# An account that orders VectorE's work charges other durations, follows a forced finish, and the conditioning loads of layer 0's pair passes are spread 6,6,6,6,1

## The chip, the cores and the metric

The kernel runs on one core of a Trainium2 chip. The metric is the device time of one launch in microseconds (us). A kernel is timed in several runs, and their median is used; beside them stands one profiled execution, whose trace gives all the durations below.

TensorE (PE) multiplies matrices, VectorE (DVE) and ScalarE (ACT) do elementwise work, GpSimd (POOL) does next to nothing here, and SyncE's queue (SP) issues almost all transfers. Each engine works through its own queue in order and waits where an instruction needs something that is not there yet.

## The reference

Two layers over 1024 prompt rows and 32 rows of a running stream, with `D_MODEL` = 1024 and `D_FF` = 4096, all in float32:

```python
for i in range(DEPTH):                                   # DEPTH = 2
    mod = jax.nn.silu(c) @ w_ada[i] + b_ada[i]           # conditioning
    sh1, sc1, gt1, sh2, sc2, gt2 = jnp.split(mod[:, None, :], N_MOD, axis=-1)
    h = rmsnorm(x, g_norm[i, 0]) * (1 + sc1) + sh1
    if i % N_MIXERS == 0:                                # layer 0
        mix, v = sgu_mixer(h, ...)
    else:                                                # layer 1
        mix = pool_mixer(h_ext, L, pool_w_grp[j], pool_scale[j])
    x = x + gt1 * rmsnorm(mix, g_norm[i, 1])
    h = rmsnorm(x, g_norm[i, 2]) * (1 + sc2) + sh2
    f = jnp.square(jax.nn.relu(h @ ffn_w_up[i])) @ ffn_w_down[i]
    x = x + gt2 * rmsnorm(f, g_norm[i, 3])
```

The pooling mixer of layer 1 takes trailing means over 2, 4, 8 and 16 rows, subtracts the row itself and multiplies by a 256x256 matrix for each of four groups.

## The kernel before

**Tiles.** The rows are cut into three tiles (`TILES`): tile 0 and tile 1 of 384 rows, tile 2 of 256 prompt rows and the 32 stream rows (288 columns). Activations are held transposed, features on the partitions. Every float32 product is made of three matmuls: each operand is split into a high part (`wh`, `hh`, `fh`; a copy by ScalarE) and a low part (`wl`, `hl`, `fl`; a subtraction by VectorE), and `products` (L1042 ff.) issues high*high, high*low and low*high. So each 128x1024 piece of weights costs one transfer of 512 KB into one of three `raw` buffers, one ScalarE copy and one VectorE subtraction before TensorE may use it.

**Passes.** The channel MLP runs in passes (`passes`): a layer, a first chunk `c` of 512 hidden features, the tiles, and the number of chunks taken together. In layer 0: two passes of tile 0, three of tile 1, five passes c = 3 to 7 of tiles 0 and 1 together (the pair passes, `pair_item`; their up-projection has seven block products in place of eight, with operands that `combos` prepares), and four passes of tile 2 with two chunks each. Layer 1 is alike: a pass of tile 0, two of tile 1, six pair passes c = 2 to 7, four passes of tile 2. Up-projections write the tiles `pf` (`pfa`, `pfb`, `pfc` in pair passes), down-projections write `pg`, which VectorE adds to `acc`.

**The conditioning.** `w_ada` comes in pieces of 512 KB too, through the same `raw` buffers and in the same stream of loads as the weights. `do_ada` multiplies and adds a piece on VectorE (instructions `aa<-raw,csil,aa`); every four pieces of a column block end in two transposes and two sums (`part`), and a small matmul (`ada`, L649) folds the sums. The list `rest` holds the pieces that are still to come; `some_ada(n)` puts the next n of them into the stream. After the weights of each pair pass of layer 0 five pieces are put in, after those of layer 1 two (L422).

**Fillers.** The work between the matmuls of one stage and the next is written as generators in the list `fillers`: the residual and its norm (`residual`, `Stat`), the pooling (`to_pool`), the modulation (`modulate`, `apply`), `combos`. `pull` runs the next step of the first or second filler. For layer 1, `ffn1_0` and `ffn1_1` take tile 0 and tile 1 from the end of the last pair pass of layer 0 to the operands `hh` and `hl` of layer 1's first passes: residual of layer 0 (statistics `pn_r2_0_0x` and `pn_r2_0_1x` on TensorE), windows on VectorE (`win`), matmuls `pp` (L1940), their norm (`pn_rp`), a second residual (`pn_r1_1_0x`, `pn_r1_1_1x`), and the modulation. In the trace the statistics of the second residual are `pn_r_0x` and `pn_r_1x`. While these run, TensorE has the four passes of tile 2 of layer 0.

**The account.** The program is written out in one order for each engine when it is built, and that order is decided by two running sums in `time`. `tick` adds the matmuls' time to `time["pe"]`; every VectorE operation issued through `tt`, `stt`, `ts` or `turn32` adds a fixed time and its elements divided by a rate to `time["dve"]` (L71 to L87). `weave`, called after each group of matmuls, takes a step of the weight stream unless `stream_waits` holds it back (for weights not needed soon, where fillers are there and `dve` is over 1.0 ahead of `pe`; for conditioning, 0.5 ahead), and then pulls fillers while `dve` is behind `pe`. A filler that waits for something gives a number, and `pull` opens it again only once `pe` has come to the larger of the two sums plus that number. Folds of the conditioning are put off in the same way (`defer`).

**Forced finishes.** Where a stage needs a filler's result, `finish(tag)` (L816) pulls until that filler is done, whatever the account says; so do `run_ffn` before the first pass of each tile and `pair_item` (for `combos`, and for tile 2 ahead of the down-projection of the last pair pass).

Of the kernel before, what the change touches and what calls it, by code (L numbers as in the profile page):

```python
# [35 lines left out]
def tile_stream_encoder_step(  # L36
# [25 lines left out]
    nc = tc.nc  # L62
# [5 lines left out]
    time = {"pe": 0.0, "dve": 0.0}  # L68
# [5 lines left out]
    def on_dve(op, fixed, rate):  # L74
        def run(out, *args, **kw):
            n = 1
            for k in out.shape[1:]:
                n *= k
            time["dve"] += fixed + n / rate
            return op(out, *args, **kw)  # L80

        return run

    tt = on_dve(nc.vector.tensor_tensor, 0.16, 930.0)
    stt = on_dve(nc.vector.scalar_tensor_tensor, 0.16, 840.0)
    ts = on_dve(nc.vector.tensor_scalar, 0.1, 930.0)
    turn32 = on_dve(nc.vector.transpose, 0.1, 930.0)  # L87

    def pool(name, **kw):
        return ctx.enter_context(tc.tile_pool(name=name, bufs=1, reuse_waits="tile", **kw))  # L90
# [52 lines left out]
    def ps_ms(name):  # L143
        return psum.tile([P, 512], F32, tag="pm", bufs=3, name=name)
# [207 lines left out]
    def w_chunk(n):  # L352
        l, c, tiles, m = passes[n]
        for j in range(4 * m):
            f = 4 * c + j
            add_w(
                ("up", n, j),
                ffn_w_up[l][:, f * P : (f + 1) * P].rearrange("(k p) f -> p k f", p=P),
                (8, P),
                ("one", "two")[j % 2] if tiles == PAIR else "w",  # L360
            )
        w = 256 // m
        for q in range(4 * m):
            add_w(
                ("dn", n, q),
                ffn_w_down[l][c * 512 : (c + m) * 512, q * w : (q + 1) * w].rearrange(
                    "(j p) d -> p j d", p=P
                ),
                (4 * m, w),
            )  # L370
# [15 lines left out]
    def some_ada(n):  # L386
        for _ in range(min(n, len(rest))):
            add, l, j = rest.pop(0)
            add(l, j)
# [29 lines left out]
    for n, (l, c, tiles, m) in enumerate(passes):  # L419
        w_chunk(n)  # L420
        if tiles == PAIR:
            some_ada((5, 2)[l])  # L422
        elif l == 0 and tiles != [NT - 1] and c > 0:
            some_ada(c + 1 if tiles == [1] else 2)
    some_ada(99)
# [120 lines left out]
    def ada_finish(l, sl, view):  # L546

        nk = 2 * view.shape[1]
        m = mod[:, l, 2 * sl : 2 * sl + nk, :].rearrange("p (s h) v -> p s h v", h=2)
        b = bT[:, l * 48 + 2 * sl : l * 48 + 2 * sl + nk].rearrange("p (s h) -> p s h", h=2)  # L550
        tt(out=m, in0=view, in1=b.unsqueeze(3).broadcast_to([P, nk // 2, 2, NV]), op=ALU.add)
        which, k0 = sl // 4, 2 * (sl % 4)
        slot = {1: (0, 0), 2: (1, 1), 4: (2, 2), 5: (3, 3)}.get(which)
        if slot is not None:
            cf, gi = slot
            for v in range(NV):
                stt(
                    out=coef[:, l, cf, v, k0 : k0 + nk],
                    in0=mod[:, l, 2 * sl : 2 * sl + nk, v],
                    scalar=1.0 if cf in (0, 2) else 0.0,  # L560
                    in1=g_of(l, gi)[:, k0 : k0 + nk],
                    op0=ALU.add,
                    op1=ALU.mult,
                )
# [40 lines left out]
    def do_ada(l, sl, q, r, w):  # L605
        nq = w // 128
        if q == 0:
            aas = [
                work.tile([P, 512], F32, tag="aa", bufs=2, name=f"aa{l}_{sl}_{w}_{i}")
                for i in range(nq // 2)  # L610
            ]
            ada_acc[0] = [aas[v * nq // 4][:, v * w % 512 :][:, :w] for v in range(NV)]
        aa = ada_acc[0]
        for c in range(8 // nq):
            for v in range(NV):
                x = r[:, c * w : (c + 1) * w]
                k = csil[:, 8 // nq * q + c, v : v + 1]
                if q == 0 and c == 0:
                    with tc.issue_after(last_lo[("v", 1, 3)].ins):
                        ts(aa[v], x, k, None, op0=ALU.mult)  # L620
                else:
                    stt(out=aa[v], in0=x, scalar=k, in1=aa[v], op0=ALU.mult, op1=ALU.add)
        if q < nq - 1:
            return


        ns = nq // 2
        i = sl * ns % 4
        if i == 0 and state["folds"]:
            run_deferred(True)  # L630
        for v in range(NV):
            turned = r[:, v * w : (v + 1) * w]
            turn32(turned, aa[v])
            time["dve"] += 0.16 + w / 840.0
            nc.vector.tensor_reduce(
                out=part[:, i : i + ns, v],
                in_=turned.rearrange("p (s b m) -> p s b m", s=ns, m=32),
                op=ALU.add,
                axis=AX.X,
            )  # L640
        if i + ns < 4:
            return
        state["folds"] = 1

        def fold():
            state["folds"] = 0
            pa = ps_ms(f"ada{l}_{sl}")
            for c in range(4):
                mm(  # L649
                    pa[32 * c : 32 * c + 32, :16],  # L650
                    quad,
                    part.rearrange("p s v (h c) -> p c (s v h)", c=4)[:, c],
                    start=True,
                    stop=True,
                    tile_position=(0, 32 * c),
                    skip_group_check=True,
                )
            y = pa[:, :16].rearrange("p (s v h) -> p s h v", s=4, v=NV)
            ada_finish(l, (sl + 1) * ns - 4, y)

        defer(fold, fold_lag[0])
# [3 lines left out]
    def defer(step, us=None):  # L665

        at = 0.0 if us is None else max(time["pe"], time["dve"]) + us
        deferred.append((at, step))

    def run_deferred(force=False):  # L670
        n = len(deferred)
        while n > 0 and (force or deferred[0][0] <= time["pe"]):
            deferred.pop(0)[1]()
            n -= 1
# [39 lines left out]
    def stream_step():  # L714
# [17 lines left out]
        if kind == "w":  # L732
            do_w(key, r)
        elif kind == "wide":
            do_ada(*key, r, 512)
        elif kind == "ada":
            if k < first_ada:
                do_ada_pe(*key, r)
            else:
                do_ada(*key, r, 256)  # L740
        else:
            do_x(key, r)
# [35 lines left out]
    def pull(force=False):  # L778

        def open_(f):
            return force or gates.get(f[0], 0.0) <= time["pe"]

        if sticky:
            f = sticky[-1]
            if not open_(f):
                return False
            sticky.pop()
        else:  # L790
            f = next((f for f in list(fillers)[:2] if open_(f)), None)
            if f is None:
                return False
        try:
            step = next(f[1])
        except StopIteration:
            fillers.remove(f)
            return True
        if step is True:
            sticky.append(f)  # L800
        elif step is not False:
            gates[f[0]] = max(time["pe"], time["dve"]) + step
        return True
# [12 lines left out]
    def finish(tag):  # L816
        while any(f[0] == tag for f in fillers):
            pull(True)


    def spread(t, ss, tag, out, dg):
# [729 lines left out]
    def pair_item(p, after, ends):  # L1551
# [48 lines left out]
        def up(jp):  # L1600
# [10 lines left out]
            if jp == 0:  # L1611
                flush()
                finish("combos")
# [56 lines left out]
        if passes[p + 1][2] != PAIR:  # L1670
            finish(f"ffn{l}_{NT - 1}")
            fillers.append(late_norm.pop())
# [277 lines left out]
    def run_ffn(l, after):  # L1950
        for p, (pl, c, tiles, m) in enumerate(passes):
            if pl != l:
                continue
            ends = [t for t in tiles if not any(q[0] == l and t in q[2] for q in passes[p + 1 :])]
            if tiles == PAIR:
                pair_item(p, after, ends)
                continue
            for t in tiles:
                if c == 0:
                    if any(f[0] == f"ffn{l}_{t}" for f in fillers):  # L1960
                        flush()
                    finish(f"ffn{l}_{t}")
                ffn_item(p, t, after if t in ends else None)
# [158 lines left out]
```

## Time and profile before

| what | value |
|---|---|
| median of 3 runs | 2157.3 us (2157.04 to 2158.1) |
| the profiled execution, its time | 2154.9 us |
| the profiled execution, its span | 2153.1 us |
| instructions in the span | 32925 |
| DVE busy | 1560.3 us, 72% of the span |
| ACT busy | 1041.6 us, 48% of the span |
| DMA read and written | 274.76 MB and 30.66 MB |

The span runs from the first to the last instruction of the trace; the execution's own time is 1.8 us longer. Times in the views are counted from the start of the span. In the view of waits each row names who waited, for whom, the sum in us, how often, and the longest. In the view of windows each row has the stretch, its length and then for each engine the busy time with the number of instructions, the clock granted to TensorE as a share of full speed, and the DMA engines' share and rate. In the timeline each row has start, duration, engine, line, operation, tiles and shapes. VectorE's and TensorE's instructions overlap a little: the distance from one start to the next is shorter than the duration of one.

### The profile page before, as it was taken

The numbers are of one execution on the slowest core, as the hardware profiler recorded it, in microseconds if no ns is written. First come the engines' busy times: TensorE is split into PE (matmuls) and PEld (weight loads), VectorE is DVE, ScalarE is ACT, GpSimd is POOL, SyncE is SP. The second block draws the span as 40 slices with busy tenths as digits, with TensorE's granted clock in tenths as the row PEclk, the third lists the DMA queues.
The fourth block names the chain that finished last, engine by engine and source line by source line (L and its number), as shares of the span: only waits on it lengthen the run. The fifth ranks groups of instructions, "written<-read, shape, count | busy, mean of one in ns | idle before, by whom it ended". The sixth has DMA issues, their size and how long they took to land.

```text
span 2153.1 us, 32925 instructions
## 1 busy us (share of the span) xinstructions
PE 2102.8 (98%) x12858; PEld 2032.5 (94%) x12858; DVE 1560.3 (72%) x2756; ACT 1041.6 (48%) x1833; POOL 22.4 (1%) x44
## 2 busy tenths in 40 slices
PE   8999999999999999999998999896999999999998
PEld 6878999999999999999998999896999999999998
DVE  6778837567778857878777887849677768579554
ACT  5634431233456545334455756555445454365555
POOL 0000000000000000000000000000000000001100
PEclk9999999999999999999999999998999999999999
DMA  8576524353445443334335775643342323238873
GB/s 290 169 256 210 179 81 136 97 163 109 122 129 167 138 147 121 105 98 128 108 122 146 214 221 145 191 131 104 89 142 90 91 86 101 69 113 224 203 188 92
DMA packets 424050, 307.59 MB, mean 143 GB/s; under 512 B 47023, under 2 KB 387287, under 8 KB 423893
## 3 DMA queue, kind: packets, MB, share of 16 engines
q1 hardware_dynamic: 422964, 304.19, 47.2%
q8 instruction: 101, 1.65, 0.3%
q0 software_dynamic: 896, 1.28, 0.2%
q14 instruction: 57, 0.46, 0.1%
q10 hardware_dynamic: 32, 0.01, 0.0%
HBM read 274.76 MB, written 30.66 MB: 142 GB/s over the span
## 4 chain that ended last, share of the span: by engine, by line
PE 90%; DVE 5%; DMA 2%; ACT 2%; issue 1%; DVEq 0%; ACTq 0%
PE pg L1048 10%; PE pg L1047 10%; PE pg L1049 10%; PE pf L1047 5%; PE pf L1048 5%; PE pf L1049 5%; PE pu L1047 3%; PE pu L1049 3%; PE pu L1048 3%; PE po L1047 3%; PE po L1049 3%; PE po L1048 3%; PE pfa L1586 3%; PE pfa L1588 3%; PE pfa L1587 3%; PE pv L1073 2%
## 5 line engine op out<-in xcount | busy, mean ns | idle before, releaser
L1047 PE MATMUL pg<-fh,wh_dn 128*128 128x384 f32 (+1 forms) x968 | 314.7, 326 | 0.9 <-DVE acc L80 0.9
L1048 PE MATMUL pg<-fl,wh_dn 128*128 128x384 f32 (+1 forms) x968 | 312.9, 323 | 0.0
L1049 PE MATMUL pg<-fh,wl_dn 128*128 128x384 f32 (+1 forms) x968 | 311.9, 323 | 0.0
L80 DVE TENSOR_TENSOR wl_dn<-raw,wh_dn 128x1024 fp32r<-128x1024 f32 x148 | 181.1, 1224 | 140.3 <-ACT wh_dn L533 92.9
L1047 PE MATMUL pf<-hh,wh_up 128*128 128x288 f32 (+1 forms) x832 | 262.4, 316 | 10.0 <-ACT hh L1007 8.4
L1048 PE MATMUL pf<-hl,wh_up 128*128 128x288 f32 (+1 forms) x832 | 260.8, 314 | 0.0
L1049 PE MATMUL pf<-hh,wl_up 128*128 128x288 f32 (+1 forms) x832 | 260.1, 313 | 0.0
L533 ACT ACTIVATE wh_dn<-raw 128x1024 fp32r<-128x1024 f32 x148 | 156.7, 1059 | 152.2 <-PE pf L1048 65.1
L80 DVE SCALAR_TENSOR_TENSOR aa<-raw,csil,aa 128x512 f32<-128x512 f32 (+1 forms) x364 | 206.2, 620 | 4.5 <-DMA raw<-in_w_ada_dram 4.4
L80 DVE TENSOR_TENSOR acc<-acc,pg 128x384 f32<-128x384 f32 (+1 forms) x256 | 134.7, 531 | 85.7 <-PE pg L1049 84.4
L1047 PEld LDWEIGHTS pg<-fh,wh_dn 128*128 128x128 f32 x968 | 181.5, 188 | 2.6 <-DVE acc L80 1.3
L1048 PEld LDWEIGHTS pg<-fl,wh_dn 128*128 128x128 f32 x968 | 181.7, 188 | 1.0 <-DVE fl L80 0.2
L1049 PEld LDWEIGHTS pg<-fh,wl_dn 128*128 128x128 f32 x968 | 181.6, 188 | 0.0
L533 ACT ACTIVATE wh_up<-raw 128x1024 fp32r<-128x1024 f32 x104 | 110.2, 1059 | 127.1 <-PE pg L1048 76.2
L80 DVE TENSOR_TENSOR wl_up<-raw,wh_up 128x1024 fp32r<-128x1024 f32 x104 | 126.8, 1220 | 61.1 <-ACT wh_up L533 60.6
L1047 PEld LDWEIGHTS pf<-hh,wh_up 128*128 128x128 f32 x832 | 158.5, 191 | 12.6 <-ACT hh L1007 9.2
L1048 PEld LDWEIGHTS pf<-hl,wh_up 128*128 128x128 f32 x832 | 158.4, 190 | 1.1 <-DVE hl L80 0.9
L1049 PEld LDWEIGHTS pf<-hh,wl_up 128*128 128x128 f32 x832 | 158.8, 191 | 0.1
L1047 PE MATMUL pg<-fx,wh_dn 128*128 128x288 f32 (+1 forms) x392 | 121.8, 311 | 0.0
L1048 PE MATMUL pg<-fx,wh_dn 128*128 128x288 f32 (+1 forms) x392 | 121.7, 311 | 0.0
L1049 PE MATMUL pg<-fx,wl_dn 128*128 128x288 f32 (+1 forms) x392 | 121.4, 310 | 0.0
L1047 PE MATMUL po<-ush,wh_o 128*128 128x384 f32 (+1 forms) x288 | 92.6, 322 | 0.0
(408 smaller groups left out, 5112.3 us busy)
## 6 DMA issues: line engine op xcount, KB each, us to landing
raw<-in_ffn_w_up_dram SPq DMA_DIRECT2D x148, 512.0 KB, 4.0
raw<-in_ffn_w_down_dram SPq DMA_DIRECT2D x148, 512.0 KB, 4.1
raw<-in_w_ada_dram SPq DMA_DIRECT2D x90, 512.0 KB, 4.2
raw<-in_sgu_w_in_dram SPq DMA_DIRECT2D x40, 512.0 KB, 4.0
xd<-acc SPq DMA_DIRECT2D x8, 1536.0 KB, 7.4
raw<-in_sgu_w_out_dram SPq DMA_DIRECT2D x24, 512.0 KB, 3.6
xo_r<-xd SPq DMA_DIRECT2D x32, 384.0 KB, 4.1
vd<-vt SPq DMA_DIRECT2D x32, 256.0 KB, 4.4
```

Of the source, the lines that this page charges most:

```text
L80: return op(out, *args, **kw)
L533: act(out=wh, in_=r, func=AF.Copy)
L1047: mm(ps[:, :n], wh, rh, start=i == 0, stop=False)
L1048: mm(ps[:, :n], wh, rl, start=False, stop=False)
L1049: mm(ps[:, :n], wl, rh, start=False, stop=i == last)
L1073: mm(ps[:m, :], a_h, wh[:, o : o + 512], start=k == 0, stop=False)
L1586: mm(ps[:, :n], wh[:, o], rh, start=first and k == 0, stop=False, skip_group_check=True)
L1587: mm(ps[:, :n], wh[:, o], rl, start=False, stop=False, skip_group_check=True)
L1588: mm(ps[:, :n], wl[:, o], rh, start=False, stop=k == HK - 1, skip_group_check=True)
```

## The change

The account's charges become 0.07 + n/950 for `tensor_tensor` (n elements per partition), 0.13 + n/950 for `scalar_tensor_tensor`, 0.13 + n/1900 for `tensor_scalar` and 0.06 + n/880 for the transpose; the `part` sums are charged 0.06 + n/950. For 1024 columns the subtraction's charge goes from 1.261 to 1.148 us, for 512 columns the multiply-add's from 0.770 to 0.669 us. After a forced finish `pe` is set to at least `dve` less 3.0. And the pair passes c = 3, 4, 5 and 6 of layer 0 put in six pieces of conditioning each and the pass c = 7 one, 25 in all as before; layer 1 keeps two. No operation or transfer of the kernel is added or removed; what changes is the order in which the instructions of each engine are written out, and with it ScalarE's function table is loaded 18 times where it was 16.

```diff
-    tt = on_dve(nc.vector.tensor_tensor, 0.16, 930.0)
-    stt = on_dve(nc.vector.scalar_tensor_tensor, 0.16, 840.0)
-    ts = on_dve(nc.vector.tensor_scalar, 0.1, 930.0)
-    turn32 = on_dve(nc.vector.transpose, 0.1, 930.0)
+    tt = on_dve(nc.vector.tensor_tensor, 0.07, 950.0)
+    stt = on_dve(nc.vector.scalar_tensor_tensor, 0.13, 950.0)
+    ts = on_dve(nc.vector.tensor_scalar, 0.13, 1900.0)
+    turn32 = on_dve(nc.vector.transpose, 0.06, 880.0)
...
         if tiles == PAIR:
-            some_ada((5, 2)[l])
+            some_ada(2 if l else 6 if c < 7 else 1)
...
             turn32(turned, aa[v])
-            time["dve"] += 0.16 + w / 840.0
+            time["dve"] += 0.06 + w / 950.0
...
     def finish(tag):
         while any(f[0] == tag for f in fillers):
             pull(True)
+        time["pe"] = max(time["pe"], time["dve"] - 3.0)
```

## The prediction

> **What bounds the kernel now.** The page first: TensorE is busy almost all the time, so only what makes it wait, or slows it, can be won.
>
> ```profile
> span 2153.1 us, 32925 instructions
> PE 2102.8 (98%) x12858; PEld 2032.5 (94%) x12858; DVE 1560.3 (72%) x2756; ACT 1041.6 (48%) x1833; POOL 22.4 (1%) x44
> ```
>
> Some 50 us of the span are idle. The view of waits, for TensorE alone, names what ended them.
>
> ```profile
> PE pn_r_1x L920 <- ACT sc_r_1x L873: 12.5, 1, 12.5
> PE pf L1047 <- ACT hh L1007: 8.4, 2, 4.3
> PE ada L649 <- DVE part L635: 5.8, 2, 5.5
> ...
> PE pn_r_0x L920 <- ACT sc_r_0x L873: 3.1, 1, 3.1
> ...
> PE pf L1047 <- ACT wh_up L533: 1.4, 2, 0.7
> PE pfa L1586 <- ACT wh_up_A L491: 1.3, 1, 1.3
> ```
>
> `pn_r_0x` and one `hh` wait are the entry of tile 0 into layer 1, `pn_r_1x` and the other that of tile 1: 3.1 + 12.5 + 8.4 = 24.0 us in which TensorE has nothing left to do and the filler has not come through. The 5.5 us are a fold of conditioning that stands on TensorE's queue ahead of sums VectorE has not made. The timelines of both engines show it:
>
> ```profile
> 1145.89 0.29 PE L1048 MATMUL pf<-hl,wh_up 128*128 128x288 f32 x1
> 1151.69 0.31 PE L649 MATMUL ada<-part,quad 128*32 128x16 f32 x8 [5.50 <-DVE part L635]
> ```
>
> ```profile
> 1146.94 0.55 DVE L80 TENSOR_TENSOR acc<-acc,pg 128x384 f32<-128x384 f32 x1
> 1147.41 0.74 DVE L80 SCALAR_TENSOR_TENSOR aa<-raw,csil,aa 128x512 f32<-128x512 f32 x1
> 1148.08 0.56 DVE L80 TENSOR_TENSOR sq_rf<-sq_rf 128x384 f32<-128x384 f32 x1
> 1148.56 1.30 DVE L80 STREAM_TRANSPOSE raw<-aa 128x512 f32<-128x512 f32 x2
> ...
> 1150.27 1.27 DVE L635 TENSOR_REDUCE part<-raw 128x16 f32<-128x512 f32 x2
> ```
>
> Each of the three stops also costs time afterwards. The view by windows, behind each:
>
> ```profile
> 1152.00:1157.00 5.00, 5.00 (x20) 5.00 (x21) 2.45 (x6) 1.55 (x2) 0.00 (x0) 0.51 0.80 224
> 1157.00:1162.00 5.00, 5.00 (x40) 5.00 (x39) 3.36 (x4) 3.94 (x7) 0.00 (x0) 1.00 0.76 215
> 1380.00:1386.00 6.00, 6.00 (x19) 5.56 (x20) 5.99 (x12) 3.00 (x6) 0.00 (x0) 0.54 0.12 35
> 1386.00:1391.00 5.00, 5.00 (x30) 5.00 (x30) 2.26 (x3) 2.78 (x6) 0.00 (x0) 1.00 0.00 0
> 1479.00:1485.00 6.00, 6.00 (x21) 5.64 (x20) 6.00 (x12) 3.00 (x6) 0.00 (x0) 0.54 0.00 0
> ```
>
> The granted clock is 0.51 to 0.54 after each. In 5 us TensorE does 20 matmuls where it then does 40: 2.5 us lost. In 6 us it does 19 and 21 where 30 in 5 us would give 36: 2.8 and 2.5 us. Together 7.8 us.
>
> Whether VectorE has room to do the fillers earlier, and the matmuls' pace, is in four longer windows:
>
> ```profile
> 950.00:1000.00 50.00, 50.00 (x290) 50.00 (x290) 35.45 (x55) 23.20 (x43) 0.00 (x0) 1.00 0.34 106
> 1150.00:1300.00 150.00, 148.07 (x1099) 147.49 (x1100) 118.59 (x163) 93.62 (x153) 0.00 (x0) 0.98 0.72 210
> 1313.00:1373.00 60.00, 58.19 (x412) 55.38 (x410) 59.25 (x89) 41.51 (x71) 0.00 (x0) 1.00 0.65 193
> 2000.00:2050.00 50.00, 50.00 (x379) 49.90 (x378) 26.37 (x32) 25.51 (x39) 5.84 (x10) 1.00 0.79 198
> ```
>
> While TensorE works on tile 2 from 1150 to 1300, VectorE is busy 118.59 of 150 us, 79%; from 1313 to 1373 it is full, 59.25 of 60, and TensorE still loses under 2 us. The work is there to be moved from the full stretch into the slack one. A matmul of 384 columns takes 50/290 = 0.172 us, one of 288 columns 50/379 = 0.132 us.
>
> **The change part by part.** The two built programs have the same matmuls, VectorE operations and transfers; what stands where differs, and I read it from the changed program's order. VectorE's work I add up by start-to-start distances, from its full stretch:
>
> ```profile
> 1341.71 0.46 DVE L80 TENSOR_TENSOR fx<-r,fx 128x288 fp32r<-128x288 f32 x1
> 1342.08 0.97 DVE L80 TENSOR_TENSOR win1p<-win1p 128x786 f32<-128x786 f32 x1
> 1342.97 0.55 DVE L80 SCALAR_TENSOR_TENSOR r_rp<-q_rp,r_rp 128x384 f32<-128x384 f32 x1
> ...
> 1345.82 0.95 DVE L80 SCALAR_TENSOR_TENSOR acc<-win1p,acc 128x768 f32<-128x768 f32 x1
> 1346.69 0.61 DVE L80 SCALAR_TENSOR_TENSOR acc<-acc,coef,r_rp 128x384 f32<-128x384 f32 x1
> 1347.22 1.22 DVE L80 TENSOR_TENSOR wl_dn<-raw,wh_dn 128x1024 fp32r<-128x1024 f32 x1
> 1348.35 0.45 DVE L80 TENSOR_TENSOR fl<-r,fh 128x288 fp32r<-128x288 f32 x1
> ```
>
> That is 0.37 us for 288 columns, 0.89 for a window, 0.87 for 768 columns, 0.53 for a multiply-add of 384 and 1.13 for a weight's low part; the fences above give 0.47 for an addition of 384 and 0.67 for a multiply-add of 512. The new charges are these distances (1.148 for the weight, where the old account had 1.261), so the account finds VectorE behind TensorE more often and draws fillers earlier.
>
> *Entry into layer 1.* `pn_r1_1_0x` now stands 408 matmuls of 288 columns and 22 of 384 ahead of the first `pf1_0_0` (408 x 0.132 + 22 x 0.172 = 57.6 us), `pn_r1_1_1x` 386 of 384 columns ahead of the first `pf1_0_1` (66 us); before, only the statistics' own few matmuls lay between. Behind such a statistic VectorE owes 2 + 16 multiply-adds, 18 x 0.53 = 9.5 us, ScalarE eight copies beside them: covered several times over. Removed: 24.0 us.
>
> *The last fold of conditioning.* With one piece left for c = 7, the sums of `ada1_9` now precede that pass's first addition of `pg`, and its fold stands 156 matmuls of 384 columns earlier. Removed: 5.5 us. In its place one matmul of `pf0_0_2_0` stands there ahead of it and waits for a weight copy; 0 to 1.3 us, part of the pass-start term below.
>
> *The clock.* Without the three stops the 7.8 us of half clock go as well. Removed in all: 24.0 + 5.5 + 7.8 = 37.3 us.
>
> *New waits.* I laid VectorE's instructions end to end from the last place where its queue runs empty, against TensorE's matmuls from the same place. On the order of before such a sum gives 10.9 us for the recorded 12.5 and 4.8 for the 5.5.
>
> (a) Tile 2 of layer 0. From the read of `pg0_2_2_4` to `fl0_4_2_7`: 12 weights (13.6), 17 multiply-adds of 384 (9.0), 12 of 288 columns (4.4), 10 windows (8.9), 7 of 768 columns (6.1), 4 additions of 384 (1.9), a copy: 44.0 us. TensorE needs it after 294 matmuls of 288 columns (38.8), 8 of the pooling, and 2 more (0.3): the row
>
> ```profile
> 1302.45 2.58 PE pp L1940 x8
> ```
>
> adds 2.6, 41.7 in all. VectorE is 2.3 us late, and everything of layer 0's `acc` and `fl` queues behind it. Bounds 0 (ScalarE and TensorE interleave) and 4.4, if the 2.1 us by which `sm_rp_0` is late come on top; I take 2.3, since the full stretch above let TensorE lose 1.8 us in 60.
>
> (b) The first matmuls of `pfb1_3_0` are written into the down-projection of pass c = 2 of layer 1, 38 matmuls of 384 columns (6.5 us) behind `pg1_2_0_1`. Their weight `S31` comes behind five additions of 384 (2.4), four multiply-adds of 512 (2.7), three halves of a weight at some 0.6 (1.8), one weight (1.1) and nine short pieces at 0 to 0.37: 8.0 to 11.3, late by 1.5 to 4.8; I take 3.3, the middle. What is late next are the matmuls `pp2` behind it. After it the clock may fall: 0 or 2.6 us (the mean above), and as the waits of 0.7 and 1.3 us left it at 1.00 while 3.1 + 4.1 lowered it, I take 2.6.
>
> (c) The gating stage. Ahead of `usl1_0_1` 22.5 us stand on VectorE's queue against 20.7 on TensorE's, ahead of `usl5_2_1` 13.6 against 12.3: 1.8 + 1.3 = 3.1. ScalarE switches its table twice more, by this row at 1.28 us each:
>
> ```profile
> L1389 ACT ACT_TABLE_LOAD x3 | 3.8, 1283 | 0.1
> ```
>
> Bounds 0 and 3.1 + 2.6 = 5.7; I take 3.1, as ScalarE has half its time free.
>
> (d) Starts of the pair passes. A sixth piece is four multiply-adds and a quarter of two transposes and two sums, 2.7 + 0.6 = 3.3 us of VectorE ahead of the next pass's weights. Beside TensorE's 1.3 us above, ScalarE waits there for a transfer:
>
> ```profile
> ACT wh_up_A L491 <- DMA raw<-in_ffn_w_up_dram: 66.1, 9, 15.5
> ```
>
> Four starts: at worst 13.2, at best the present 1.3 + 1.4 go (-2.7); I take 1.5, near the wait that is recorded.
>
> Sum: -37.3 + 2.3 + 3.3 + 2.6 + 3.1 + 1.5 = -24.5 us. The profiled execution took 2154.9 us (span 2153.1 and 1.8 around it), which gives 2130.4; it lies 2.4 below the median of the runs shown, 2157.3, and on that scale I forecast 2133 us. With every added term at its bound: 37.3 + 2.7 gained is 2117; 4.4 + 4.8 + 2.6 + 5.7 + 13.2 = 30.7 added is 2151.
>
> The row says that a stop of 5.5 us or more costs about 2.6 us afterwards. The Trainium skill, "TensorE: Matmul & The Clock Gate", Part 1, has the clock fall to half after an idle window of about 3.4 us that runs free of the kernel, and rise after one busy window. An estimate from its figure would put 1.7 us on each stop, 5.1 for the three, and the forecast at about 2135; against the change it says that (b), at 3.3 us, may or may not lower the clock. Here the trace shows 2.5 to 2.8, and the trace decides.
>
> **The rivals.** *No new wait counts* (0.15): small waits are taken up by what lies around them, as the order of before had some of 2 to 3 us in tile 2's passes that no row shows. 2157.3 - 37.3 = 2120. Against it: an earlier stop of TensorE had cushioned those.
>
> *The pair passes start late* (0.17): the sixth piece holds the `raw` buffers, and four starts cost 3.3 us more each, the bound in (d); 13.2 - 1.5 = 11.7 more than forecast, 2145. For it: 66.1 us of ScalarE waiting for these transfers. Against it: TensorE has shown only 1.3 us of that.
>
> *VectorE cannot be filled so far* (0.10, slower). From `pn_rf0_0` to `pg0_4_2_7` its queue holds 147.1 us against 1104 matmuls of 288 columns and 20 of the pooling, 152 us. If it does no more than the 79% of 1150 to 1300, because it stands waiting for ScalarE's copies, the stretch takes 147.1/0.79 = 186: 34 us more in place of (a), -37.3 + 34 + 10.5 = +7, 2164. It decides against the change below 147.1/(152 + 26.8) = 0.82. For it: 79% is what these very passes show over 150 us. Against it: 59.25 of 60 with the same kinds of work.
>
> *It moves nothing that counts* (0.06): the stops reappear elsewhere at the same price, 2157. Against it: at the entry the built order leaves 57 us where there was nothing.
>
> **How the numbers follow.** The forecast has 0.52, with 2125 to 2142 as its own range, half way to either end. The range 2117 to 2151 takes in the bounds and the first two rivals and leaves out the slower one and most of the last. A run can be told from no change at 0.2%, 4.3 us: faster holds 0.52 + 0.15 + 0.17 = 0.84, the same 0.06, slower 0.10.
>
> **What would show it.** Right: `pn_r_0x`, `pn_r_1x` and both `hh` waits gone from TensorE's rows, no `ada` wait above 1 us, granted clock 1.00 from 1150 to 1500; VectorE busy over 90% from 1150 to 1300. Wrong: waits of `pg` for `fl` that add up to over 10 us there (VectorE not filled), `pfa` for `wh_up_A` four times (starts), or a wait of `pfb` in layer 1 far above 4 us.

## The result, and the profile after

The changed kernel takes 2132.66 us (median of four runs, 2132.16 to 2136.42) where the kernel before takes 2157.7 beside it (2157.04 to 2158.65): a ratio of 0.9887, with a 95% interval of 0.987 to 0.9905. That is 25.0 us less. The changed file has one line more from L817 on, so that L1047 of before is L1048 here.

The first lines of the profile's page, span and busy times:

```profile
span 2130.7 us, 32913 instructions
PE 2098.8 (99%) x12858; PEld 2025.9 (95%) x12858; DVE 1556.3 (73%) x2756; ACT 1039.4 (49%) x1835; POOL 22.3 (1%) x44
```

TensorE's busy time hardly moves (2102.8 before); the span loses 22.4 us and TensorE's idle time goes from 50 us to 32. The view of TensorE's waits in the changed kernel, from 960 to 1700 us (who waited, for whom, us in total, times, longest):

```profile
PE pfb L1587 <- ACT wh_up_S L508: 3.9, 1, 3.9
PE pfa L1587 <- ACT a L1593: 1.6, 1, 1.6
PE pg L1048 <- DVE acc L80: 1.1, 3, 0.7
PE pg L1048 <- ACT fx L1308: 1.0, 1, 1.0
PE pg L1048 <- ACT combo_R L1308: 0.9, 1, 0.9
PE pg L1049 <- DVE fl L80: 0.5, 2, 0.3
PE pp L1941 <- DMA wg<-in_pool_w_grp_dram: 0.4, 1, 0.4
PE pg L1049 <- DVE fx L80: 0.4, 1, 0.4
...
```

(Three rows of 0.2 us each are left out at the end.) The rows `pn_r_0x`, `pn_r_1x` and `pf` for `hh` are gone, and none of `ada` is left in this stretch. What stands first is new: a stop of 3.9 us of `pfb`. The view by windows, in the same columns as before, shows where VectorE's work went and where TensorE now loses:

```profile
1150.00:1300.00 150.00, 148.09 (x1054) 142.26 (x1053) 136.63 (x198) 105.41 (x181) 0.00 (x0) 1.00 0.67 201
```

```profile
1100.00:1200.00 100.00, 99.70 (x665) 99.11 (x664) 85.80 (x143) 69.81 (x133) 0.00 (x0) 1.00 0.56 168
1200.00:1300.00 100.00, 98.09 (x683) 92.46 (x682) 91.07 (x132) 67.45 (x115) 0.00 (x0) 1.00 0.66 199
1300.00:1400.00 100.00, 99.79 (x673) 95.05 (x672) 84.39 (x128) 67.39 (x113) 0.00 (x0) 1.00 0.65 192
1400.00:1500.00 100.00, 100.00 (x577) 99.50 (x576) 67.89 (x100) 58.39 (x102) 0.00 (x0) 1.00 0.52 153
1500.00:1600.00 100.00, 93.00 (x507) 87.82 (x506) 76.11 (x156) 47.44 (x94) 0.00 (x0) 0.98 0.30 85
```

VectorE is busy 136.63 of 150 us from 1150 to 1300, 91% where it was 79%. From 1100 to 1500 the clock is 1.00 and TensorE idle for 2.4 us in all. From 1500 to 1600 it is idle for 7 us, and the granted clock falls to 0.98 on the mean. The timeline of TensorE there (start, duration, and in brackets the idle time before and what ended it):

```profile
1537.71 0.34 PE L1587 MATMUL pfc<-hh,wh_up_A 128*128 128x384 f32 x1
1539.65 0.44 PE L1587 MATMUL pfa<-combo_R,wh_up_S 128*128 128x384 f32 x1 [1.60 <-ACT a L1593]
...
1554.34 0.33 PE L1050 MATMUL pg<-fh,wl_dn 128*128 128x384 f32 x1
1555.57 0.45 PE L1048 MATMUL pg<-combo_R,wh_dn 128*128 128x384 f32 x1 [0.90 <-ACT combo_R L1308]
...
1560.23 0.34 PE L1050 MATMUL pg<-combo_R,wl_dn 128*128 128x384 f32 x1
1564.45 0.44 PE L1587 MATMUL pfb<-hh,wh_up_S 128*128 128x384 f32 x1 [3.88 <-ACT wh_up_S L508]
```

And VectorE's own timeline in front of it, with ScalarE's row for the copy that TensorE waits for:

```profile
1544.00 1.22 DVE L80 TENSOR_TENSOR wl_dn<-raw,wh_dn 128x1024 fp32r<-128x1024 f32 x1 [0.55 <-PE pfb L1588]
...
1546.08 1.23 DVE L80 TENSOR_TENSOR wl_dn<-raw,wh_dn 128x1024 fp32r<-128x1024 f32 x1 [0.39 <-issue]
...
1548.14 1.22 DVE L80 TENSOR_TENSOR wl_dn<-raw,wh_dn 128x1024 fp32r<-128x1024 f32 x1 [0.37 <-ACT wh_dn L533]
...
1555.55 0.56 DVE L80 TENSOR_TENSOR combo_R<-r,combo_R 128x384 fp32r<-128x384 f32 x1 [0.80 <-ACT combo_R L1308]
...
1556.19 2.73 DVE L80 SCALAR_TENSOR_TENSOR aa<-raw,csil,aa 128x512 f32<-128x512 f32 x4
...
1562.29 0.68 DVE L80 TENSOR_TENSOR raw<-raw,raw 128x512 f32<-128x512 f32 x1
```

```profile
1563.06 1.33 ACT L508 ACTIVATE wh_up_S<-raw 128x512 fp32r<-128x512 f32 x2 [7.55 <-DVE raw L80]
```

ScalarE stands idle for 7.55 us because the sum `raw` that it is to copy comes from VectorE at 1562.29, behind four multiply-adds of conditioning, a weight's low part, additions of `pg` and window pieces. And VectorE, which the account takes to be busy without a break, has itself waited in this stretch: 0.55 + 0.39 + 0.37 + 0.80 = 2.1 us, for TensorE, for the issue and for ScalarE.

### The profile page after: what moved, and what is told of

The parts are those of the page before. It is cut to its first block, busy times and chain, and to the rows that moved or that the text cites. A ratio compares the mean times of both kernels' runs of the same rounds, so it can differ in the third digit from the quotient of the medians.

```text
span 2130.7 us, 32913 instructions
## 1 busy us (share of the span) xinstructions
PE 2098.8 (99%) x12858; PEld 2025.9 (95%) x12858; DVE 1556.3 (73%) x2756; ACT 1039.4 (49%) x1835; POOL 22.3 (1%) x44
## 4 chain that ended last, share of the span: by engine, by line
PE 60%; DVE 5%; DMA 2%; ACT 1%; issue 1%; SPq 0%; DVEq 0%; ACTq 0%
PE pg L1049 10%; PE pg L1048 10%; PE pg L1050 10%; PE pf L1048 5%; PE pf L1049 5%; PE pf L1050 5%; PE pfa L1587 2%; PE pfa L1589 2%; PE pfa L1588 2%; PE pfb L1589 1%; PE pfb L1587 1%; PE pfb L1588 1%; PE pp L1941 1%; DMA raw<-in_ffn_w_up_dram 1%; DVE aa L80 1%; DVE acc L80 1%
## 5 line engine op out<-in xcount | busy, mean ns | idle before, releaser
L1048 PE MATMUL pg<-fh,wh_dn 128*128 128x384 f32 (+1 forms) x968 | 314.1, 325 | 1.3 <-DVE acc L80 1.3
L1048 PE MATMUL pf<-hh,wh_up 128*128 128x288 f32 (+1 forms) x832 | 259.7, 312 | 1.4 <-ACT wh_up L533 1.4
L1048 PEld LDWEIGHTS pg<-fh,wh_dn 128*128 128x128 f32 x968 | 181.7, 188 | 3.2 <-DVE acc L80 2.2
L1048 PEld LDWEIGHTS pf<-hh,wh_up 128*128 128x128 f32 x832 | 156.0, 188 | 2.9 <-ACT wh_up L533 2.5
L1048 PE MATMUL pg<-fx,wh_dn 128*128 128x288 f32 (+1 forms) x392 | 122.9, 314 | 1.0 <-ACT fx L1308 1.0
L1048 PE MATMUL po<-ush,wh_o 128*128 128x384 f32 (+1 forms) x288 | 92.7, 322 | 0.0
```

Source lines behind the costliest of these rows:

```text
L1048: mm(ps[:, :n], wh, rh, start=i == 0, stop=False)
```

## Experiments

The kernels were timed in three rounds, four of them at a time, beside the kernel before; its median was 2156.52 us beside e1 to e4, 2156.63 beside e5 to e8 and 2154.93 beside e9 to e12.

| kernel | us (median) | ratio to before, 95% interval |
|---|---|---|
| e1_charges: new charges alone | 2129.01 | 0.9878, 0.9863 to 0.9893 |
| e2_finish: catch-up alone | 2125.45 | 0.986, 0.9845 to 0.9875 |
| e3_spread: 6,6,6,6,1 alone | 2128.31 | 0.9873, 0.9857 to 0.989 |
| e4_no_charges: catch-up and spread | 2115.46 | 0.9813, 0.9798 to 0.9827 |
| e5_no_spread: charges and catch-up | 2128.84 | 0.9871, 0.9856 to 0.9885 |
| e6_l1_old: all, old charges in layer 1 | 2120.05 | 0.9831, 0.9816 to 0.9846 |
| e7_sgu_old: all, old charges up to layer 0's passes | 2131.66 | 0.9887, 0.9873 to 0.9902 |
| e8_scale110: e4 with charges of 110% | 2145.38 | 0.9954, 0.9938 to 0.9971 |
| e9_l0_new: e4 with new charges in layer 0's passes | 2115.6 | 0.9816, 0.9801 to 0.9831 |
| e10_reserve1: all, fillers held 1 us back | 2117.76 | 0.9827, 0.9812 to 0.9842 |
| e11_half: e4 with charges half way to the new | 2115.87 | 0.982, 0.9805 to 0.9835 |
| e12_scale095: e4 with charges of 95% | 2116.59 | 0.9825, 0.9808 to 0.9841 |

**The parts, one at a time and two at a time.** The edits are the hunks of the change itself: e1 has the five lines of charges, e2 the line in `finish`, e3 the line with `some_ada`, e4 the last two, e5 the first two.

> The new charges alone, with five pieces per pair pass and no catch-up. Theory (the charges draw the fillers earlier): the three stops of TensorE before the change (5.5, 7.2 and 16.8 us, with 7.8 us of half clock) are gone, the small new waits of the gating stage (about 1 to 3 us) are there as in the changed kernel, and the sum of the built order leaves up to 2.7 us at the first weights of a pair pass of layer 1: 2128 to 2140 us. Rival (the spread of the conditioning or the catch-up does it): over 2148 us.

> The catch-up after a forced finish alone, with the old charges and five pieces. Theory that the stops at the entry of layer 1 come from an account that lags after forced finishes: by the built order the statistics of both tiles come ahead of their use, so the 24.0 us and their half clock go without the new waits of the gating stage: 2120 to 2132 us. Rival (only the charges move the fillers): 2150 to 2158 us.

> The spread 6,6,6,6,1 alone, with the old charges and no catch-up. Theory (less VectorE work at the last pair pass lets the whole chain start earlier): the 5.5 us fold and its half clock go, and the chain of tile 0 and tile 1 arrives some 12 to 15 us earlier at the entry of layer 1, so that of 24.0 us some 5 to 10 stay: 2128 to 2142 us. Rival (the spread touches the fold alone): 2149 us, 8 less than before.

> Catch-up and spread together, with the old charges: the change without its charges. If the gain is all in the removed stops and the new charges only bring the new waits (gating stage, tile 2's passes, the block of weights of pass c = 3 in layer 1), it is as fast as the changed kernel or faster, 2118 to 2130 us, with no wait of TensorE above 2.5 us after the start. Rival (the new charges are what the gain comes from): 2140 us or more.

> New charges and catch-up, the old spread of five pieces for every c. The catch-up alone took 2125.5 us; with the spread it took 2115.5 and with charges and spread 2132.7. Theory (the parts remove the same stops, and the new charges then cost what they make late, which the two programs' queues decide): the stops at the entry stay away, and the queue sums put VectorE late by 2.7 us at one weight copy of layer 1, 3.3 at sm_rp_0, 3.9 at fl0_4_2_7, 1.9 + 1.3 in the gating stage, while S31 is no longer late: 2125 to 2131, near the new charges alone (2129.0). Rival (the new charges cost a fixed 17.2 us beside any other part): 2125.5 + 17.2 = 2142.7. Second rival (the new charges cost only together with the spread): 2125 or below, with no new wait of pfb, pf or pg over 1.5 us.

Each part by itself gains 27.5 to 31.1 us, more than the three together. The gains are not shares of the change: each one alone makes the fillers start early enough that the stop of 12.5 us at `pn_r_1x` is gone. The longest wait that is left in each, after the first 60 us, from the view of TensorE's waits. In e1:

```profile
PE pfa L1588 <- DVE wl_up_A L80: 2.9, 1, 2.9
```

In e2:

```profile
PE pf L1048 <- ACT r L1501: 2.1, 1, 2.1
```

In e3, where alone a long row of the old stops remains:

```profile
PE pf L1047 <- ACT hh L1007: 5.4, 2, 4.3
```

e4, without the new charges, beats the kernel before by 41.1 us and the changed one by 17.2. Its waits from 960 to 1700 us come to 2.3:

```profile
PE pg L1048 <- DVE acc L80: 1.2, 2, 1.0
PE pg L1049 <- DVE fx L80: 0.9, 1, 0.9
PE pn_rp L921 <- ACT sx_rp L874: 0.2, 1, 0.2
```

So with the other two parts in place the new charges cost 17.2 us. They don't cost that beside any part: on top of the catch-up alone it is 3.4 us (e5 against e2), which rules out a fixed price. One part of the change does nothing here. Built with new charges and spread but without the catch-up, the program has the same instructions in the same order on every engine as the changed kernel (read from the two built programs, not from a run). Beside the old charges the catch-up does work: it takes 12.9 us off the spread alone (e4 against e3).

**Where the 17.2 us are.** In e6 the charges are switched to the old ones where layer 1's passes begin; in e7 the old ones hold until layer 0's passes begin; in e9 the new ones hold in layer 0's passes alone. The edit of e6, with the two tables of values written here as `new` and `old`:

```diff
+    charges = dict(new)
+    later = dict(old)
...
-            time["dve"] += fixed + n / rate
+            time["dve"] += charges[name][0] + n / charges[name][1]
...
+    charges.update(later)
     run_ffn(1, to_out)
```

> The changed kernel, with the old charges from the start of layer 1's passes on. Theory (the new charges cost most in layer 1, where S31 comes late and all of 1500 to 1600 us with it, 11 us beyond the pace of the stretches around): the wait of pfb for wh_up_S and the half clock behind it go, 2121 to 2123, and the waits of 0.5 to 1 us in the gating stage and at pg of tile 2 stay. By the prediction's own term for it, 3.3 + 2.6 = 5.9: 2127. Rival (the loss in that stretch is set by how full tile 2's passes of layer 0 leave VectorE, and not by the charges of layer 1): pfb or its like still waits over 3 us, 2131 to 2133.

> The changed kernel, with the old charges up to the start of layer 0's passes and the new ones after it. Theory: the wait of psp and the copies of the gating stage come in time again, and the two more table loads go, 2 to 3 us less than the changed kernel, 2129.7 to 2130.7; the prediction's term is 3.1, 2129.6. The wait of pfb for wh_up_S stays at 3 to 5 us. Rival (the 17 us of the new charges come from the gating stage, by what it leaves standing in front of the passes): 2116 to 2120, with pfb's wait gone.

> Catch-up and spread, with the new charges in layer 0's passes alone and the old ones in the gating stage and in layer 1. Theory (the 17 us between the program without the new charges, 2115.5, and the changed kernel, 2132.7, are a sum of places: 12.6 in layer 1, 1.0 in the gating stage, and what is left, 3.6, in layer 0's passes, where the profile of the changed kernel shows waits of 1.0, 0.5 and 0.4 us at tile 2): 2117 to 2119.5. Rival (the losses of layer 0's passes come only with those of the gating stage before them): 2115 to 2116.5.

e6 takes 12.6 us less than the changed kernel. Its window from 1500 to 1600, to be held against the one of the changed kernel above, has no gap, and the view of waits has no row in it:

```profile
1500.00:1600.00 100.00, 100.00 (x581) 99.49 (x580) 78.81 (x146) 48.79 (x97) 0.00 (x0) 1.00 0.29 85
```

So most of the loss is in layer 1. e7 takes 1.0 us less, and the rival that put all of it into the gating stage falls: the row of `pfb` stands as it was, and of the changed kernel's waits over 0.2 us only this one is gone (view of waits of the changed kernel, 60 to 960 us):

```profile
PE psp L1402 <- DVE aa L80: 1.2, 1, 1.2
```

In e9 the theory was wrong and its rival right: 2115.6 us, nothing over e4's 2115.5. The new charges in layer 0's passes fill VectorE as far as in the changed kernel, and cost nothing by themselves:

```profile
1200.00:1300.00 100.00, 97.74 (x682) 92.31 (x681) 90.45 (x129) 66.25 (x113) 0.00 (x0) 1.00 0.66 198
```

From e6 to e9 only the gating stage's charges differ, and that is 4.4 us, where e7 gave 1.0 for the same edit; from e9 to e7 only layer 1's charges differ, and that is 16.1 us, where e6 gave 12.6. Either way the steps from e4 to the changed kernel add up to the 17.2, as they must; the medians don't say which split is right, and the runs of one kernel differ by 1.6 to 3.4 us in these three.

The profiled executions say it more finely. Take for each matmul the time from its start to the next one's start, less what it takes when nothing holds it up (0.133 us for 288 columns, 0.173 for the others), and add up. From 60 to 700 us the changed kernel loses 2.0 us more than e7, and e6 2.6 more than e9: the gating stage. From 1500 to 1700 us the changed kernel loses 12.0 more than e6, and e7 12.2 more than e9: layer 1. Against e4 the changed kernel, whose span is 16.4 us longer, loses 2.1 from 60 to 700, 0.9 from 700 to 1500, 12.4 from 1500 to 1700, and 1.2 in the first 60 us, where its mean clock is lower. This row is the changed kernel's:

```profile
0.00:60.00 60.00, 50.92 (x331) 37.19 (x332) 38.75 (x114) 35.22 (x66) 2.88 (x10) 0.97 0.79 265
```

This one is e6's, whose program is the same up to layer 1, so the 1.2 us do not come from the order that the charges give there:

```profile
0.00:60.00 60.00, 51.36 (x337) 37.86 (x338) 40.08 (x116) 36.63 (x70) 2.89 (x10) 1.00 0.81 266
```

**The level of the charges.** e8, e11 and e12 have catch-up and spread with the old charges times 1.1, half way to the new ones, and times 0.95. e10 is the changed kernel with one edit:

```diff
-        while time["dve"] < time["pe"] and fillers:
+        while time["dve"] < time["pe"] - 1.0 and fillers:
```

> Catch-up and spread with the old charges, each made 10% larger. Theory (a charge above VectorE's own pace leaves a reserve, but only as far as the entry of each tile into layer 1 is still covered): VectorE falls out of step earlier, fillers are drawn later, and the queue sums bring the entry of tile 1 back: 9.7 to 13.4 us late at its statistics and at hl, with 2.5 us of half clock behind it: 2127 to 2132. Rival (larger charges are only a larger reserve): 2115 to 2117, no wait over 1.5 us.

> The changed kernel with its new charges, in which a filler is drawn only while the account has VectorE more than 1 us behind TensorE. Theory (what the new charges take away is a reserve, and S31 comes late because the fillers keep VectorE's queue full to the last): S31 is in time again and the 12.6 us go, while the queue sums put VectorE 2 us later than in the changed kernel at tile 2 of layer 0 (6.0 in place of 4.0): 2120 to 2125. Rival (the charges cost by the proportions between kinds of instruction, not by their level): the wait of pfb for wh_up_S stays, 2130 to 2135.

> Catch-up and spread, each charge half way from the old to the new value. Theory (a place is lost only where VectorE's queue runs over TensorE's): the queue sums have S31 in time and VectorE late by 3.8 us at fl0_4_2_7 and 3.4 at sm_rp_0: 2117 to 2121, no wait of pfb over 2 us. Rival (the loss grows evenly with the charge): half way between 2115.5 and 2132.7, 2124.

> Catch-up and spread with the old charges, each made 5% smaller. Theory (ten per cent more uncovers the entry of tile 1 and cost 30 us; less than the old charges takes reserve away at single places, here 2.0 and 2.1 us by the queue sums): 2115 to 2119. Rival (the time falls further with smaller charges until the new ones): below 2114.

With 10% more the entry of tile 1 is uncovered again, and it costs 29.9 us against e4, about twice what the queue sums gave. In its waits the two old rows come back, and a third, `pn_rf`, beside them:

```profile
PE pn_r_1x L921 <- ACT sc_r_1x L874: 11.6, 1, 11.6
PE pf L1048 <- ACT hh L1008: 7.0, 2, 3.6
...
PE pn_rf L921 <- ACT sc_rf L874: 3.1, 1, 3.1
```

The expectation priced one stop and one half clock; there are three kinds of wait (11.6 + 7.0 + 3.1 = 21.7 us), and the windows of e8 show the clock fall behind them, to 0.95 and 0.91 on the mean:

```profile
1300.00:1400.00 100.00, 93.03 (x601) 88.52 (x600) 83.87 (x124) 65.10 (x112) 0.00 (x0) 0.95 0.54 160
1400.00:1500.00 100.00, 84.13 (x438) 77.61 (x437) 71.97 (x111) 55.56 (x96) 0.00 (x0) 0.91 0.39 117
```

Below the old charges there is a flat stretch: 95% and half way give 2116.6 and 2115.9, against 2115.5 (the intervals of their ratios overlap). Then it ends: the full new charges give 2132.7. The loss doesn't grow evenly with the charge (half way would have been 2124). And e10 gives 14.9 of the 17.2 us back with the new charges kept, by holding every filler 1 us; its waits from 1500 to 1600:

```profile
PE pg L1048 <- DVE acc L80: 1.0, 1, 1.0
PE pp L1941 <- DMA wg<-in_pool_w_grp_dram: 0.7, 1, 0.7
```

The stop of `pfb` is gone. So most of the loss lies in the level of the account against the real queue, and not in the proportions between kinds of instruction, which e10 leaves as the change made them. That the 2.1 us which VectorE waits in that stretch are what the reserve has to cover is argued from the timeline, not shown by a run: the prediction's sum for (b), which counts no wait of VectorE, already has the weight 1.5 to 4.8 us late, so the order alone may be enough. The best of all the versions is e4, level with e9, e11 and e12.

Several expectations had the right side and a range that was too narrow: e4 came out 2.5 us below its range, e6 1.0 below, e10 2.2 below, e11 1.1 below and e7 1.0 above. In each of them the rival was further off. In e8 the size was half of what came, and in e9 the theory itself was wrong.

## Why the prediction was right, and where its terms were not

The forecast of a net -24.5 us stands against a measured -25.0. Behind it are two terms that were both some 5 to 6 us too small by the medians and cancel, so that it came within 0.5 us is luck. e4, the change without its charges, gains 41.1 where the prediction's removed sum and pass starts give 37.3 - 1.5 = 35.8; the charges then give back 17.2 where terms (a), (b) and (c) give 2.3 + 5.9 + 3.1 = 11.3.

*Removed stops.* Right by their rows: both statistics, both `hh` waits and the fold of `ada` are gone, and the clock is 1.00 from 1100 to 1500. The size was less short than the medians have it. The spans of the two profiled executions differ by 38.8 us (2153.1 and 2114.3), and by the sum over matmul starts all of it goes between 1100 and 1500 us (38.9; the rest cancels), against 37.3 for stops and half clock. Part of these 1.6 us is how a row counts: from the end of the matmul in front, 0.33 us after its start, where the next one could start 0.17 us after it, so each stop is some 0.16 us longer than its row. The other 2.3 of the 41.1 are the distance between profiled executions and medians.

*The cause given for the removed stops* was the charges, which find VectorE behind and draw fillers earlier. They do that (e1), but the catch-up and the spread do it as well without them (e2, e3, e4). The trace of before could not tell which of three parts, each nearly sufficient, was needed.

*(a) Tile 2 of layer 0.* 2.3 forecast. In the changed kernel `pg` waits there for `fx` (1.0 and 0.4) and `fl` (0.5): 1.9 us. The rival of a VectorE that can't be filled decided below 82%; it was 91%, and that rival falls. e9 adds that the filling costs next to nothing by itself against e4, which has waits of its own there.

*(b) `pfb1_3_0`.* Place, operand and wait were right: 3.88 us against 3.3 (called the middle of 1.5 and 4.8, which is 3.15). The half clock behind it was 1.7 against 2.6:

```profile
1564.00:1566.00 2.00, 1.45 (x4) 1.01 (x5) 1.97 (x5) 0.40 (x1) 0.00 (x0) 0.70 0.06 13
1566.00:1568.00 2.00, 2.00 (x6) 1.56 (x6) 0.69 (x1) 0.00 (x0) 0.00 (x0) 0.50 0.34 118
1568.00:1570.00 2.00, 2.00 (x9) 1.60 (x8) 0.00 (x0) 0.47 (x1) 0.00 (x0) 0.95 0.00 0
```

(0.30 x 2 + 0.50 x 2 + 0.05 x 2 = 1.7 us at the windows' mean clocks.) The step that failed is that the stretch was given this one stop, 5.9 us in all. Three more waits stand in it, 1.60 ahead of `pfa`, 0.90 ahead of `pg` for a `combo_R`, 0.44 ahead of `pp`: 6.8 us of waits in all, 8.5 with the half clock, and 12.6 when the charges of layer 1 are undone. Laying VectorE's instructions end to end counts neither VectorE's own waits nor the copies that ScalarE makes between two of its steps. The sum over matmul starts gives 12.0 for 1500 to 1700: 8.2 at waits that have a row, three short ones behind 1600 us among them, 1.8 in the half clock, and 2.0 in gaps too small for a row.

*(c) The gating stage.* 3.1 forecast; 1.0 and 4.4 by the medians, 2.0 and 2.6 by the profiled executions, as said above. That VectorE comes late there is right: the wait for it goes with the old charges (e7), and ScalarE's table loads go from 18 back to 16. The place is another: it is `psp` that waits, 1.2 us, and the changed kernel has no row for `usl`.

*(d) Starts of the pair passes.* 1.5 forecast. One wait of `pfa` for `wh_up_A` is left, 1.2 us, where four were the rival's sign, and it was 1.3 before; that rival falls. By the sum over matmul starts the changed kernel loses 1.0 us more than the kernel before in the pair passes (835 to 1140 us) and 1.1 more than e5, which keeps five pieces.

*"No new wait counts"*, 2120, did not happen to this change, but it is nearly what e4 is without the new charges (2115.5).

## What to carry to other kernels

An account that orders one engine's work against another's is not bound to get better by being made as exact as the instructions' own spacing. Here such charges gained 27.5 us alone, and cost 17.2 beside the other two parts, most of it at one place that came late and paid with more than its own wait; 1 us of reserve gave 14.9 of them back. That exact charges leave nothing for the times that the engine itself waits is the likely reason, and is not shown. Charges too large were worse (10% more cost 30 us), so it pays to try the level of an account by itself, or an explicit reserve, on both sides. And where a change has several parts, run each alone: three parts that each nearly suffice look like a sum when they are only run together.

## What the runs showed of the hardware

A stop does not have to be long to halve TensorE's clock. After the 2.14 us wait in e2 the windows read:

```profile
1219.00:1221.00 2.00, 0.10 (x1) 0.10 (x1) 2.00 (x5) 2.00 (x5) 0.00 (x0) 0.94 0.28 66
1221.00:1223.00 2.00, 2.00 (x9) 2.00 (x10) 2.00 (x4) 2.00 (x6) 0.00 (x0) 0.50 0.75 209
1223.00:1225.00 2.00, 2.00 (x13) 2.00 (x13) 2.00 (x6) 1.97 (x5) 0.00 (x0) 0.71 0.82 243
```

That is 0.12 + 1.0 + 0.58 = 1.7 us lost, as much as behind the 3.88 us of the changed kernel, while the 1.60 us at 1538 left the clock at 1.00. After 2.9 us in e1 the clock stayed low twice as long:

```profile
1644.00:1646.00 2.00, 0.42 (x1) 0.42 (x2) 2.00 (x4) 0.00 (x0) 0.00 (x0) 0.69 0.10 29
1646.00:1648.00 2.00, 2.00 (x8) 2.00 (x8) 2.00 (x4) 0.94 (x2) 0.00 (x0) 0.50 0.80 233
1648.00:1650.00 2.00, 2.00 (x8) 2.00 (x7) 1.93 (x4) 0.32 (x1) 0.00 (x0) 0.50 0.05 8
1650.00:1652.00 2.00, 2.00 (x9) 2.00 (x8) 0.90 (x2) 0.00 (x0) 0.00 (x0) 0.61 0.00 0
```

0.62 + 1.0 + 1.0 + 0.78 = 3.4 us, of which 0.4 fall before the next matmul starts at 1645.58 and cost nothing: 3.0 lost. The low clock comes in pieces of 3.4 us, so 1.7 us of work each, and the length of the wait alone does not say how many. The Trainium skill, "TensorE: Matmul & The Clock Gate", Part 1, has windows of about 3.4 us that run free of the kernel; half speed for one such window is the estimate of 1.7 us that the prediction set aside, and e2 and the changed kernel agree with it, e1 with two windows. The idle window that the prediction took from there for the clock's fall need not be a whole one, though: the stop of 2.14 us was shorter.

The 2.5 to 2.8 us behind the longer stops of before fit in as well, for there the clock falls while TensorE still waits. The view by windows gives 0.50 without a break from 1150.1 to 1156.8, two pieces, but the matmul that the stop held back starts only at 1151.69, and half of the 5.1 us from there on is 2.6 us. From 1375.4 to 1385.5 and from 1464.1 to 1484.5 it is 0.50 too, three and six pieces long, and a second wait falls into each.

Such a piece can also come without a change in the program ahead of it. In the profiled executions of the changed kernel, e5, e7 and e10 the clock is at 0.50 for 3.4 us near 20 us (18.6 to 22.0 in the changed kernel); in those of e6 and of all the others it stays at 1.00 there. What sets it is not shown.
